# Block products for six of the eight gate columns of the second half's last merge

## The chip, the cores and the metric

The kernel runs on one core of one Trainium2 chip. The core has five engines with a queue each: TensorE (PE: matmuls, with its weight loads shown as PEld), VectorE (DVE), ScalarE (ACT), GpSimd (POOL) and SyncE (SP, which here only issues DMAs). Each engine works through its own queue in order; between engines they wait on semaphores. The metric is the device time of one execution in microseconds, the median of the runs.

## The reference

One layer of a conditioned decoder runs over a prompt of 1024 tokens and over 8 samples of 4 tokens each, with shared weights and a model width of 1024. All arithmetic is in float32.

```
h = rmsnorm(x, norm1_g) * (1 + sc1) + sh1
u = h @ w_in                     # u_x, u_g, u_q, u_k, u_v, u_r, u_lr, u_ga, u_gb
y_a = rg_lru(causal_conv(u_x)) * gelu(u_g)
y_b = headnorm(gla(u_q, u_k, u_v, u_lr)) * silu(u_r)
m = sigmoid(u_ga) * (y_a @ proj_a) + sigmoid(u_gb) * (y_b @ proj_b)
x = x + gt1 * (m @ w_out)
h2 = rmsnorm(x, norm2_g) * (1 + sc2) + sh2
x = x + gt2 * ((silu(f1) * f2) @ ffn_w2)      # f1, f2 = halves of h2 @ ffn_w1
y = rmsnorm(x, final_g)
```

The change concerns the line of `m`, in it the first gate: `sigmoid(u_ga)`, where `u_ga = h @ w_in[:, ga]` has 1024 columns, that is eight tiles of 128.

## The kernel before

**Halves.** Features lie on the 128 partitions, tokens along the free dimension. The work is done in two halves one after the other: half A has 512 prompt tokens, half B the other 512 and the 32 sample tokens (544 columns, of which a matmul takes two pieces of 272). Names of tiles end in `a` or `b` accordingly.

**Split products.** A float32 matrix product is made of three passes in the type fp32r. Weights (`split_w`) and inputs (`split`) are each split into a high part (a copy by ScalarE) and a rest (a subtraction by VectorE); `gemm` adds high x high, high x rest and rest x high in PSUM. A plain gate column of half B is therefore 8 tiles of the inner dimension x 2 pieces x 3 = 48 matmuls of 272 columns; its `proj_a` column, with an inner dimension of 1280 = 10 tiles, is 60.

**Block products.** The first FFN matrix is multiplied in another way (`ffn1_fast` with `products` and `block_sums`): weights (two column tiles) and inputs (two halves of the inner dimension, two halves of the tokens) are seen as 2 x 2 blocks, and seven products of blocks, after sums on both sides, take the place of eight. The sums of the weights are made beforehand by VectorE and kept in DRAM (`weight_sums`, `late_sums`, into `wsum`), the sums of the inputs by `block_sums`: four rounds, each with two additions over all tokens, four subtractions over half of them and three splits. A round's temporaries `d0`, `d1`, `ta`, `tb` come from a pool of six buffers (tag "t"); its results `t12` and every second round's `t4` from a pool of 17 (tag "S"). The first product, "11", needs no sums of the inputs; the second, "t1", needs the `t12` of all four rounds.

**The stages of half B.** `branches` runs the attention (`gla`) with a list of other work as its fill, in this order: values of the first pair of heads, queries and keys of the second, values of the second, the `r` tiles, the LRU branch (`lru`). Then comes `merge_b` (eight columns of the second gate and of `proj_b`), with the LRU's remaining steps woven in; then `merge_a` (eight columns of the first gate and of `proj_a`); then `back`: out-projection, second norm, FFN. Between `merge_a` and `back` the PSUM pool is changed from three tiles of two banks to six of one (`mm_pool(1)`).

**The weight sums.** `late_sums` is a list of jobs, each in two steps. The first step has POOL copy one column of the tile in `pace[0]`, the latest gate, which makes its queue wait until that is written, and then issue two loads; the second has VectorE do four additions and POOL issue two stores. `merge_b` takes two steps per column from its fifth column on, `merge_a` two steps per column: 24 steps for 12 jobs.

**Order.** A scheduler orders each engine's instructions at build time, by program order and by when it expects their inputs. A piece of code under `high_priority` is moved ahead (the weight splits by 70 instructions); `as_written` fixes the order of one engine from a given place on, which the block products use for PE.

## Time and profile before

| | us |
|---|---|
| median of three runs (lowest, highest) | 1967.7 (1966.91, 1968.15) |
| the profiled execution | 1969.03 |
| span of its profile | 1967.3 |
| second merge of half B, `merge_a`: first gate matmul to first matmul of the out-projection | 1429.06 to 1539.00 |

Times in the trace are counted from the start of the span. One instruction's duration includes the time in which the next one already runs: a matmul of 272 columns is listed with some 0.29 us although the next follows after 0.12. So rates are read from start to start. A line of the profile names the line of the kernel, the engine, the tile written and the tiles read; "idle before" and the name behind an arrow say how long the engine stood still and what ended that.

### The profile page before, as it was taken

Reading aid. Unit: us, or ns where it says so; the run is one execution under the profiler, and the core shown is the slowest. Engines: PE = TensorE matmul, PEld = TensorE weight load, DVE = VectorE, ACT = ScalarE, POOL = GpSimd, SP = SyncE. Lnnn points to the kernel's source line nnn. Section 1 sums busy time; section 2 is a strip of 40 time slices with the busy share of each in tenths; the row PEclk is TensorE's granted clock in tenths of the full one; section 3 lists DMA queues with packets and bytes.
Section 4 is the critical chain, followed back from the end, with each engine's and each line's share of the span. In section 5 each row is a group of like instructions: output and inputs, shape, how many; then the busy total and the mean of one; then the engine's idle time right before and its main releaser. Section 6 shows DMA issues by size and latency. Waiting matters only on the chain. (4 is left out here: it accounts for less than half of the span.)

```text
span 1967.3 us, 33687 instructions
## 1 busy us (share of the span) xinstructions
PE 1935.1 (98%) x13428; PEld 1762.0 (90%) x13428; DVE 1320.0 (67%) x2293; ACT 942.8 (48%) x1442; POOL 107.5 (5%) x231
## 2 busy tenths in 40 slices
PE   8999999999999999999999999999999999999998
PEld 5877877777899998998899999899999999999997
DVE  5638487655558765778564597684365588888867
ACT  4645375533235542555353355563232344566653
POOL 0000001000000000000000001010221000000000
PEclk9999999999999999999999999999999999999999
DMA  8334235567644457554422313323456544555553
GB/s 340 98 106 156 81 107 193 186 229 277 219 164 143 149 187 247 179 174 142 157 76 89 116 60 108 102 82 107 135 198 216 202 135 129 173 169 179 176 163 108
DMA packets 116797, 307.68 MB, mean 156 GB/s; under 512 B 13728, under 2 KB 28832, under 8 KB 116640
## 3 DMA queue, kind: packets, MB, share of 16 engines
q1 hardware_dynamic: 104656, 260.74, 40.8%
q0 software_dynamic: 11440, 44.23, 6.1%
q8 instruction: 105, 1.72, 0.4%
q10 hardware_dynamic: 544, 0.56, 0.1%
q14 instruction: 52, 0.43, 0.1%
HBM read 271.08 MB, written 34.39 MB: 155 GB/s over the span
## 5 line engine op out<-in xcount | busy, mean ns | idle before, releaser
L151 DVE TENSOR_TENSOR fwa_hl<-fwa,fwa_hl 128x1024 fp32r<-128x1024 f32 (+1 forms) x57 | 68.8, 1206 | 44.7 <-ACT fwa_hl L150 41.2
L151 DVE TENSOR_TENSOR fwb_hl<-fwb,fwb_hl 128x1024 fp32r<-128x1024 f32 (+1 forms) x64 | 77.2, 1206 | 27.8 <-ACT fwb_hl L150 25.7
L150 ACT ACTIVATE fwa_hl<-fwa 128x1024 fp32r<-128x1024 f32 (+1 forms) x57 | 59.3, 1040 | 43.9 <-PE fapsa L1338 10.7
L150 ACT ACTIVATE fwb_hl<-fwb 128x1024 fp32r<-128x1024 f32 (+1 forms) x64 | 66.6, 1041 | 23.5 <-PE fcpsb L1338 9.1
L438 PE MATMUL f3psa<-faa,f3a_hl 128*128 128x512 f32 x176 | 68.6, 390 | 0.6 <-ACT f3a_hl L150 0.6
L440 PE MATMUL f3psa<-faa,f3a_hl 128*128 128x512 f32 x176 | 68.5, 390 | 0.4 <-DVE f3a_hl L151 0.4
L439 PE MATMUL f3psa<-faa,f3a_hl 128*128 128x512 f32 x176 | 68.6, 390 | 0.0
L150 ACT ACTIVATE f3a_hl<-f3a_raw 128x768 fp32r<-128x768 f32 (+1 forms) x32 | 25.3, 792 | 55.6 <-PE f3psa L440 47.3
L438 PE MATMUL uxpsb<-h1b,uxpsb_hl 128*128 128x256 f32 (+1 forms) x160 | 47.9, 299 | 0.1
L439 PE MATMUL uxpsb<-h1b,uxpsb_hl 128*128 128x256 f32 (+1 forms) x160 | 46.7, 292 | 0.0
L440 PE MATMUL uxpsb<-h1b,uxpsb_hl 128*128 128x256 f32 (+1 forms) x160 | 46.4, 290 | 0.0
L438 PE MATMUL ugpsb<-h1b,ugpsb_hl 128*128 128x272 f32 x160 | 46.3, 289 | 0.0
L440 PE MATMUL ugpsb<-h1b,ugpsb_hl 128*128 128x272 f32 x160 | 46.1, 288 | 0.0
L439 PE MATMUL ugpsb<-h1b,ugpsb_hl 128*128 128x272 f32 x160 | 45.8, 286 | 0.0
L438 PEld LDWEIGHTS f3psa<-faa,f3a_hl 128*128 128x128 f32 x176 | 33.1, 188 | 7.8 <-ACT f3a_hl L150 1.0
L440 PEld LDWEIGHTS f3psa<-faa,f3a_hl 128*128 128x128 f32 x176 | 33.0, 188 | 7.6 <-DVE f3a_hl L151 0.9
L151 DVE TENSOR_TENSOR f3a_hl<-f3a_raw,f3a_hl 128x768 fp32r<-128x768 f32 (+1 forms) x32 | 28.2, 887 | 16.4 <-ACT f3a_hl L150 16.3
L439 PEld LDWEIGHTS f3psa<-faa,f3a_hl 128*128 128x128 f32 x176 | 33.0, 188 | 6.7
L438 PE MATMUL wopsb<-mb,wob_hl 128*128 128x272 f32 x128 | 36.8, 288 | 1.1 <-DVE gab L1203 1.1
L438 PE MATMUL rpsb<-h1b,rpsb_hl 128*128 128x272 f32 x128 | 37.8, 295 | 0.0
L438 PE MATMUL vpsb<-h1b,vpsb_hl 128*128 128x272 f32 x128 | 37.4, 293 | 0.0
L439 PE MATMUL rpsb<-h1b,rpsb_hl 128*128 128x272 f32 x128 | 37.4, 292 | 0.0
(1134 smaller groups left out, 7739.5 us busy)
## 6 DMA issues: line engine op xcount, KB each, us to landing
ada<-in_ada_w SPq DMA_DIRECT2D x48, 512.0 KB, 6.0
fwb<-wsum SPq DMA_DIRECT2D x72, 256.0 KB, 3.4
s_raw<-in_ffn SPq DMA_DIRECT2D x32, 512.0 KB, 3.5
wsum<-s_raw POOLq DMA_DIRECT2D x32, 512.0 KB, 3.3
fwa<-wsum SPq DMA_DIRECT2D x64, 256.0 KB, 3.3
fwb<-in_ffn SPq DMA_DIRECT2D x54, 256.0 KB, 3.4
fwa<-in_ffn SPq DMA_DIRECT2D x48, 256.0 KB, 3.2
woa_raw<-in_w_out SPq DMA_DIRECT2D x13, 512.0 KB, 3.5
```

Of the source, the lines that this page charges most:

```text
L150: act.activation(hl[:, 0, :n], raw[:, :n], AF.Copy)
L151: dve.tensor_sub(hl[:, 1, :n], raw[:, :n], hl[:, 0, :n].bitcast(F32))
L438: pe.matmul(out, wh, x[:, o:o + w], start=st, stop=False)
L439: pe.matmul(out, wh, x[:, N + o:N + o + w], start=False, stop=False)
L440: pe.matmul(out, wl, x[:, o:o + w], start=False, stop=en)
```

## The change

Couples of columns (2, 3), (4, 5) and (6, 7) of half B's first gate are made by block products (`gates_fast`), columns 0 and 1 stay plain. `block_sums` now takes the tiles to be summed as an argument; for the normed input `h` its four rounds are traced one by one: behind the gate and behind the `proj_a` of columns 0 and 1. The splits of the merged columns `m` are traced later: column 0 behind column 1, columns 1 to 5 behind the last couple's gates. Three couples of gate columns add six jobs ahead of the others in `late_sums`, 18 jobs with 36 steps in all; twelve steps are taken one by one in the fill of the attention, two per column in `merge_b` from its third column on, the rest in `merge_a`. In these jobs the first addition is put behind VectorE's latest traced instruction (`behind`). The change of the PSUM pool stands at the beginning of `merge_a`. The gate tiles of `w_in` are stored with the tiles of the inner dimension in the order `KORD`, for half A as well, where they are still multiplied plainly, and half A's merge adds into `mb` in place of `ga`.

```diff
 KORD = (0, 2, 4, 6, 1, 3, 5, 7)
+GATES = (1, 2, 3)
...
     def traced():
         return nc.cur_bb.bb.instructions
+
+    def behind(n):
+
+        now = list(traced())
+        mine = [i for i in now[max(0, n - 4000):n] if i.engine == now[-1].engine]
+        order = mybir.DependencyInfo(mybir.DependencyClass.NoSync, mybir.DependencyReason.DATA)
+        tc.add_manual_dep(now[-1], mine[-1].name, order, reason="as written")
 
     def as_written(begin, engines):
 
...
     wsum = {f: drp.tile([P, 2048], F32, name=f"wsum{f}") for f in range(FAST[1], NF)}
+    wsumg = {c: drp.tile([P, 2048], F32, name=f"wsumg{c}") for c in GATES}
     wsum2 = {(q, g): drp.tile([P, 1536], F32, name=f"wsumf{q}{g}") for q in range(4) for g in range(2)}
 
     def S(name, dt=F32):
...
 
         jobs = []
         halves = lambda t, u, c: t.rearrange("p (n u) -> p n u", n=2)[:, :, c * u:(c + 1) * u]
-        for f in range(FAST[1], FAST[0]):
+        couples = [(wsumg[c], [I["w_in"][T_GA + 2 * c + v] for v in range(2)]) for c in GATES]
+        couples += [(wsum[f], [I["ffn1"][2 * f + v] for v in range(2)]) for f in range(FAST[1], FAST[0])]
+        for sums, src in couples:
             for c in range(2):
-                to = [halves(wsum[f][:, v * 1024:(v + 1) * 1024], 256, c) for v in range(2)]
-                jobs.append((256, [halves(I["ffn1"][2 * f + v], 256, c) for v in range(2)], to))
+                to = [halves(sums[:, v * 1024:(v + 1) * 1024], 256, c) for v in range(2)]
+                jobs.append((256, [halves(t, 256, c) for t in src], to))
         for g in range(2):
             for q in range(4):
                 c = P * (4 + 6 * g)
...
                 pool.dma_start(rv[v], src[v])
             yield 1
             r1, r2 = rv
+            last = len(traced())
             dve.tensor_add(r2[:, 1], r2[:, 0], r2[:, 1])
+            behind(last)
             dve.tensor_sub(r2[:, 0], r1[:, 0], r2[:, 0])
             dve.tensor_sub(r1[:, 0], r2[:, 1], r1[:, 0])
             dve.tensor_sub(r1[:, 1], r1[:, 1], r1[:, 0])
...
             yield 1
 
     sums_of, sums_late = weight_sums(), late_sums()
+
+    def paced(g, jobs):
+        for w in g:
+            next(jobs, None)
+            yield w
 
     class Half:
         def __init__(s, hf):
...
                 ps, hl = s.early.pop(t)
                 s.gemm(ps, hl, 4, s.h, 4, False, True, hk=4)
                 return ps
-            ps = mm(name)
-            s.gemm(ps, w_in_tile(t, name), KD, s.h, split=split)
+            ps = s.wide(name) if T_GA <= t < T_GB else mm(name)
+            s.gemm(ps, w_in_tile(t, name), KD, s.h, split=split, order=KORD if T_GA <= t < T_GB else None)
             return ps
 
         def by_tiles(s, dst, i, ps, func, **kw):
...
             for i in range(2):
                 ps = s.proj_h(T_Q + 2 * pr + i, f"qps{n}{i}", s.tiled)
                 s.by_tiles(q, i, ps, AF.Copy, scale=float(128 ** -0.5))
+                pace[0] = q
                 yield 5.2
             for i in range(2):
                 h = 2 * pr + i
...
             for i in range(2):
                 ps = s.proj_h(T_K + 2 * pr + i, f"kps{n}{i}", s.tiled)
                 s.by_tiles(k, i, ps, AF.Copy)
+                pace[0] = k
                 yield 5.2
             box += [z, q, k]
 
...
                     ps = s.proj_h(T_V + 4 * pr + 2 * i + c, f"vps{n}{i}{c}")
                     vf = T(f"vf{n}{i}{c}")
                     act.activation(s.sv(vf[:, :N]), s.pv(ps), AF.Copy)
+                    pace[0] = vf
                     if pend:
                         tp_(*pend)
                     pend = (i, c, vt, vs, vf)
...
                 pace[0] = tg
                 if s.hf == 0 and j:
                     next(sums_of, None)
-                elif s.hf and j >= 4:
+                elif s.hf and j >= 2:
                     next(sums_late, None)
                     next(sums_late, None)
                 yield 5.2
 
+        def over(s, t, ps):
+
+            return [(s.sv(t[:, :s.N]), s.pv(ps))] if s.hf == 0 else [(t[:, s.cols(p)], s.psv(ps, p)) for p in s.parts]
+
+        def gate_a(s, j):
+            n = f"{s.n}{j}"
+            ps = s.proj_h(T_GA + j, "gaps" + n)
+            tg = T("ga" + n)
+            for t, p in s.over(tg, ps):
+                act.activation(t, p, AF.Tanh, scale=0.5)
+            pace[0] = tg
+            return tg
+
+        def gates_fast(s, c, product):
+
+            N, W = s.N, s.N // 2
+            hi, lo = slice(0, W), slice(W, N)
+            pa, pb, pc = [mm(f"h{k}ps{s.n}{c}")[:, 0, :W] for k in "abc"]
+            v1, v2 = T(f"gc{s.n}{c}"), T(f"gd{s.n}{c}")
+            product(pa, "11", True)
+            s.snap(v1[:, lo], pa)
+            product(pb, "t1", True)
+            s.snap(v2[:, lo], pb)
+            product(pa, "t2", False)
+            s.snap(v1[:, hi], pa)
+            product(pb, "22", False)
+            product(pa, "t3", False)
+            s.snap(v2[:, hi], pa)
+            dve.tensor_add(v1[:, hi], v1[:, hi], pb)
+            product(pc, "21", True)
+            dve.tensor_add(v1[:, lo], v1[:, lo], pc)
+            dve.tensor_add(v2[:, hi], v2[:, hi], v2[:, lo])
+            act.activation(v1[:, :N], v1[:, :N], AF.Tanh, scale=0.5)
+            product(pa, "t4", False)
+            act.activation(v2[:, lo], pa, AF.Tanh, scale=0.5)
+            act.activation(v2[:, hi], v2[:, hi], AF.Tanh, scale=0.5)
+            pace[0] = v1
+            return v1, v2
+
+        def proj_a(s, j, tg):
+            n, N = f"{s.n}{j}", s.N
+            p2 = s.wide("paps" + n)
+            s.gemm(p2, load_w(I["proj_a"][2 * j], 640, "pa0" + n), 5, s.y_a, 0, True, False)
+            s.gemm(p2, load_w(I["proj_a"][2 * j + 1], 640, "pa1" + n), 5, s.y_a, 5, False, True)
+            for t, p in s.over(tg, p2):
+                dve.scalar_tensor_tensor(t, t, 1.0, p, op0=OP.add, op1=OP.mult)
+            dve.tensor_add(s.mb[j][:, :N], tg[:, :N], s.mb[j][:, :N])
+
+        def keep_m(s, *js):
+            for j in js:
+                m = S(f"m{s.n}{j}", F32R)
+                split(m, s.mb[j][:, :s.N], s.N)
+                s.m.append(m)
+
         def merge_a(s):
-            N, mb = s.N, s.mb
             s.m = []
-            for j in range(KD):
-                n = f"{s.n}{j}"
-                ps = s.proj_h(T_GA + j, "gaps" + n)
-                tg = T("ga" + n)
-                act.activation(s.sv(tg[:, :N]), s.pv(ps), AF.Tanh, scale=0.5)
-                pace[0] = tg
-                if s.hf:
+            if s.hf == 0:
+                for j in range(KD):
+                    s.proj_a(j, s.gate_a(j))
+                    s.keep_m(j)
+                    if j % 3 < 2 and j < 7:
+                        next(sums_of, None)
+                return
+            mm_pool(1)
+            b = s.block_sums(s.h, "h")
+            for j in range(2):
+                tg = s.gate_a(j)
+                next(b)
+                next(sums_late, None)
+                s.proj_a(j, tg)
+                next(b)
+                next(sums_late, None)
+            drain(b)
+            s.keep_m(0)
+            units = []
+            for c in GATES:
+                w1, w2, sm = I["w_in"][T_GA + 2 * c], I["w_in"][T_GA + 2 * c + 1], wsumg[c]
+                units += [w1[:, 0:512], sm[:, 1536:2048], sm[:, 0:512], sm[:, 512:1024], sm[:, 1024:1536], w1[:, 512:1024],
+                          w2[:, 512:1024]]
+            begin = len(traced())
+            product = s.products(units, 512, s.bs, "gw" + s.n)
+            for c in GATES:
+                tgs = s.gates_fast(c, product)
+                next(sums_late, None)
+                if c == GATES[-1]:
+                    s.keep_m(*range(1, 2 * c))
+                for i in range(2):
+                    s.proj_a(2 * c + i, tgs[i])
+                    if c == GATES[-1]:
+                        s.keep_m(2 * c + i)
                     next(sums_late, None)
-                p2 = mm("paps" + n)
-                s.gemm(p2, load_w(I["proj_a"][2 * j], 640, "pa0" + n), 5, s.y_a, 0, True, False)
-                s.gemm(p2, load_w(I["proj_a"][2 * j + 1], 640, "pa1" + n), 5, s.y_a, 5, False, True)
-                dve.scalar_tensor_tensor(s.sv(tg[:, :N]), s.sv(tg[:, :N]), 1.0, s.pv(p2), op0=OP.add, op1=OP.mult)
-                dve.tensor_add(tg[:, :N], tg[:, :N], mb[j][:, :N])
-                m = S("m" + n, F32R)
-                split(m, tg[:, :N], N)
-                s.m.append(m)
-                if s.hf:
-                    next(sums_late, None)
-                elif j % 3 < 2 and j < 7:
-                    next(sums_of, None)
+            as_written(begin, (mybir.EngineType.PE,))
 
...
-        def block_sums(s):
+        def block_sums(s, hs, tag=""):
 
             N, W = s.N, s.N // 2
             s.bs = {k: [] for k in ("11", "21", "22", "t1", "t2", "t3", "t4")}
             t3 = t4 = None
             for i in range(4):
-                h0, h1 = s.h2[2 * i], s.h2[2 * i + 1]
-                d0, d1, ta, tb = [T(f"{c}{s.n}{i}") for c in ("d0", "d1", "ta", "tb")]
+                h0, h1 = hs[2 * i], hs[2 * i + 1]
+                d0, d1, ta, tb = [T(f"{c}{tag}{s.n}{i}") for c in ("d0", "d1", "ta", "tb")]
                 for d, h in (d0, h0), (d1, h1):
                     dve.tensor_add(d[:, :N], h[:, :N].bitcast(F32), h[:, N:2 * N].bitcast(F32))
                 dve.tensor_sub(ta[:, :W], d0[:, :W], d0[:, W:N])
...
         def back(s):
             s.x, s.h2 = [], []
             p0, p1 = s.halves
-            if s.hf:
-                mm_pool(1)
             a0, a1 = [ACC("20" + s.n)], [ACC("21" + s.n)]
             drain(s.out_proj(p0, a0))
             o1 = s.out_proj(p1, a1)
...
             next(f)
             mix(s.norm2(p1, a1), f)
             drain(f)
-            b = s.block_sums()
+            b = s.block_sums(s.h2)
             if s.hf == 0:
                 mix(chain(s.ffn1_first(p1, EARLY), s.ffn1(range(EARLY, FAST[0]))), b)
                 drain(b)
...
             r = weave(s.r_tiles(), s.adas, 2)
             l = s.lru()
             fill = chain(g0, f, g1, r, l)
+            if s.hf:
+                fill = paced(fill, islice(sums_late, 4 * len(GATES)))
             mix(s.gla(0, *b0, g0, v0), fill)
             drain(f)
             mix(side(s.gla(1, *b1, g1, v1), s.head_norm(0)), fill)
...
         col(f["final_g"])], axis=1))
     w = f["w_in"][0]
     o = np.cumsum([0, 1280, 1280, 512, 512, 1024, 1024, 16, 1024, 1024])
-    a["w_in"] = _tiles(np.concatenate([w[:, :o[6]], w[:, o[7]:]], 1))
+    wi = _tiles(np.concatenate([w[:, :o[6]], w[:, o[7]:]], 1))
+    wg = wi[T_GA:T_GB].reshape(T_GB - T_GA, P, KD, P)[:, :, list(KORD)]
+    wi[T_GA:T_GB] = wg.reshape(T_GB - T_GA, P, D)
+    a["w_in"] = wi
     wl = np.zeros((P, KD, P), np.float32)
     wl[:, :, 0:16] = w[:, o[6]:o[7]].reshape(KD, P, 16).transpose(1, 0, 2)
     for o in (32, 64, 96):
```

More of the change, by code (lines that the diff above doesn't have):

```diff
@@ L1 @@
 from contextlib import ExitStack
+from itertools import islice
 import concourse.bass as bass
@@ L1300, in block_sums @@
                 if i == 0:
-                    t3 = pair(tp.tile([P, 2 * 544], F32R, tag="m2t", name="t3" + s.n, bufs=1))
+                    t3 = pair(tp.tile([P, 2 * 544], F32R, tag="m2t", name="t3" + tag + s.n, bufs=1))
                 if i == 2:
-                    t3 = [tp.tile([P, 544], F32R, tag="acc", name=f"t3{c}{s.n}", bufs=2) for c in "hl"]
+                    t3 = [tp.tile([P, 544], F32R, tag="acc", name=f"t3{c}{tag}{s.n}", bufs=2) for c in "hl"]
                 if i % 2 == 0:
-                    t4 = pair(S(f"t4{s.n}{i}", F32R))
-                t12 = pair(S(f"t12{s.n}{i}", F32R))
+                    t4 = pair(S(f"t4{tag}{s.n}{i}", F32R))
+                t12 = pair(S(f"t12{tag}{s.n}{i}", F32R))
                 o4 = i % 2 * W
```

## The prediction

> **What bounds the kernel now.** I read the page first, then the windows of the stage that the diff touches, and the time lines of TensorE, VectorE and ScalarE there.
>
> ```profile
> span 1967.3 us, 33687 instructions
> ...
> PE 1935.1 (98%) x13428; PEld 1762.0 (90%) x13428; DVE 1320.0 (67%) x2293; ACT 942.8 (48%) x1442; POOL 107.5 (5%) x231
> ```
>
> ```profile
> core 0: us, PE busy (x) PEld busy (x) DVE busy (x) ACT busy (x) POOL busy (x), PEclk, DMA share, GB/s
> 1175.00:1180.00 5.00, 4.40 (x16) 3.81 (x17) 2.63 (x7) 0.87 (x2) 0.33 (x2) 0.66 0.18 72
> 1420.00:1425.00 5.00, 5.00 (x43) 5.00 (x42) 2.37 (x4) 1.57 (x3) 1.84 (x5) 1.00 0.51 170
> 1425.00:1430.00 5.00, 5.00 (x42) 5.00 (x42) 1.36 (x4) 4.94 (x6) 1.02 (x2) 1.00 0.59 209
> 1429.00:1442.50 13.50, 13.20 (x106) 12.98 (x106) 9.95 (x20) 5.19 (x8) 4.56 (x9) 1.00 0.26 87
> 1442.50:1456.00 13.50, 13.19 (x105) 12.97 (x106) 8.87 (x12) 4.21 (x6) 4.57 (x8) 1.00 0.67 222
> 1469.30:1482.70 13.40, 13.40 (x110) 13.40 (x109) 7.01 (x10) 3.71 (x5) 2.54 (x6) 1.00 0.72 257
> 1540.00:1545.00 5.00, 5.00 (x42) 5.00 (x42) 3.02 (x5) 2.04 (x3) 0.17 (x1) 1.00 0.61 214
> 1666.00:1740.00 74.00, 74.00 (x594) 74.00 (x593) 57.64 (x93) 43.68 (x72) 0.00 (x0) 1.00 0.53 163
> 990.00:1045.00 55.00, 54.85 (x482) 53.44 (x480) 37.78 (x68) 30.09 (x53) 0.00 (x0) 1.00 0.25 76
> 1045.00:1090.00 45.00, 45.00 (x362) 42.15 (x361) 18.36 (x43) 12.15 (x21) 1.08 (x2) 1.00 0.30 98
> ```
>
> TensorE is busy in 98% of the span, so time is gained only by giving it fewer matmuls or by closing one of its gaps. Columns of the windows: length, then busy time and count of PE, PEld, DVE, ACT, POOL, then the granted clock, DMA share and GB/s. The last merge of the second half runs from 1429.06 to about 1538. From 1469 on TensorE is busy without a break while VectorE has half its time free. In the first two columns (1429 to 1456) VectorE works 18.8 us of 27, because the tail of the LRU branch runs there.
>
> ```profile
> 1429.06 0.29 PE L438 MATMUL gapsb<-h1b,gapsb_hl 128*128 128x272 f32 x1
> ...
> 1441.76 0.29 PE L438 MATMUL papsb<-yab,pa1b_hl 128*128 128x272 f32 x1
> 1442.35 0.39 PE L439 MATMUL papsb<-yab,pa1b_hl 128*128 128x272 f32 x1 [0.30 <-DVE yab L185]
> ...
> 1443.20 0.29 PE L439 MATMUL gapsb<-h1b,gapsb_hl 128*128 128x272 f32 x1
> 1443.80 0.39 PE L440 MATMUL gapsb<-h1b,gapsb_hl 128*128 128x272 f32 x1 [0.31 <-DVE gapsb_hl L151]
> ...
> 1537.62 0.29 PE L440 MATMUL papsb<-yab,pa1b_hl 128*128 128x272 f32 x1
> 1539.00 0.36 PE L438 MATMUL wopsb<-mb,wob_hl 128*128 128x272 f32 x1 [1.10 <-DVE gab L1203]
> ```
>
> ```profile
> 1490.15 0.63 ACT L1196 ACTIVATE gab<-gapsb 128x544 f32<-128x544 f32 x1 [2.04 <-PE gapsb L440]
> ...
> 1503.60 0.63 ACT L1196 ACTIVATE gab<-gapsb 128x544 f32<-128x544 f32 x1 [2.53 <-PE gapsb L440]
> ```
>
> The two tanh of consecutive columns lie 13.45 us apart. One column is 48 matmuls of 272 columns for the gate and 60 for `proj_a`: 13.45/108 = **124.5 ns** a matmul. The time line of PE shows three small gaps, which I read from start to start: 0.59 us at `yab` and 0.60 at `gapsb_hl` instead of 0.12, together 0.95 lost, and 1.38 at the first `wopsb`, on `gab`: 1.26 lost.
>
> **What the change removes.** A couple of plain gate columns is 96 matmuls; by block products it is 7 products of 4 x 3 = 84. Three couples save 36 x 0.1245 = **4.48 us**. The window 1666 to 1740 holds the same block-product structure in the first FFN matrix, with this half's 272-wide blocks: PE is busy 74.00 of 74.00 us with DVE at 57.6. So the snapshots, the additions and the 3.5 weight splits per couple (2 before) don't hold TensorE up; I price them at 0. If that cover were gone, the bound is one split's 1.14 us per product pair; the windows speak against it, since in the loop over couples VectorE has some 17 us of work in 25.4 (204 matmuls x 0.1245).
>
> The 1.26 us at the first `wopsb` goes too: it is the change of PSUM pools, which `mm_pool(1)` now makes before the stage. There the first gate must wait for the last `mbb` (0.7 us, row below); below it turns out that this is covered.
>
> **What it adds: the block sums.** They need VectorE before the second product, "t1", of the first couple, since that reads all four `t12`. Undisturbed, TensorE would reach it at 1429.06 + (216 + 12) x 0.1245 = **1457.4**. Nothing can be put ahead of it: PE's order is written down from there. What must VectorE do by then?
>
> ```profile
> 1431.52 0.42 DVE L379 TENSOR_TENSOR sums<-sums 128x256 f32<-128x256 f32 x1 [3.91 <-DMA sums<-in_ffn]
> 1431.98 0.42 DVE L380 TENSOR_TENSOR sums<-sums,sums 128x256 f32<-128x256 f32 x1
> ...
> 1433.24 0.71 DVE L1179 SCALAR_TENSOR_TENSOR mbb<-gbb,pbpsb 128x544 f32<-128x544 f32 x1
> 1433.87 1.35 DVE L1095 TENSOR_TENSOR tib<-tib,lmb 128x544 f32<-128x544 f32 x2
> ...
> 1441.57 0.72 DVE L185 TENSOR_TENSOR yab<-ggb,yab 128x544 fp32r<-128x544 f32 x1 [0.72 <-ACT yab L184]
> 1442.52 1.23 DVE L151 TENSOR_TENSOR gapsb_hl<-gapsb_raw,gapsb_hl 128x1024 fp32r<-128x1024 f32 x1 [0.22 <-ACT gapsb_hl L150]
> 1443.66 0.82 DVE L151 TENSOR_TENSOR pa0b_hl<-pa0b_raw,pa0b_hl 128x640 fp32r<-128x640 f32 x1
> ...
> 1460.60 0.56 DVE L379 TENSOR_TENSOR sums<-sums 128x384 f32<-128x384 f32 x1 [5.39 <-DMA sums<-in_ffn]
> 1461.19 0.56 DVE L380 TENSOR_TENSOR sums<-sums,sums 128x384 f32<-128x384 f32 x1
> 1462.86 0.71 DVE L1203 SCALAR_TENSOR_TENSOR gab<-gab,papsb 128x544 f32<-128x544 f32 x1
> 1463.49 0.82 DVE L151 TENSOR_TENSOR pa1b_hl<-pa1b_raw,pa1b_hl 128x640 fp32r<-128x640 f32 x1
> 1464.22 0.72 DVE L1204 TENSOR_TENSOR gab<-gab,mbb 128x544 f32<-128x544 f32 x1
> ```
>
> ```profile
> L1294 DVE TENSOR_TENSOR d0b<-h2b 128x544 f32<-128x544 f32 x4 | 2.9, 715 | 0.0
> ...
> L1311 DVE TENSOR_TENSOR t12b<-tab,t12b 128x544 fp32r<-128x544 f32 x4 | 2.9, 715 | 0.0
> ...
> L1296 DVE TENSOR_TENSOR tab<-d1b,tab 128x272 f32<-128x272 f32 x4 | 1.7, 433 | 0.0
> ...
> L1311 DVE TENSOR_TENSOR t4b<-tbb,t4b 128x272 fp32r<-128x272 f32 x4 | 1.7, 430 | 0.0
> ```
>
> Rows overlap by about 0.08 us (a 715 ns addition is followed 0.63 us later), so I count start to start. Block sums, from the four rounds in the FFN: per round 3 operations of 0.715 and 6 of 0.43 us (`d1b`, `tbb` and `t3b` are as wide as the rows shown); four rounds are 12 x 0.715 + 24 x 0.43 = 18.9 less 36 x 0.08 = 16.0 us; without the last t3 and t4, which t1 doesn't need, **15.3**. Beside them stand, from 1429.3 (last `pbpsb` written): the last `mbb` 0.64; one job of weight sums, four times 0.59 = 2.4; the LRU tail, 1433.87 to 1442.29 less a `pa1b` split (0.74) and an idle 0.72 = 7.0; the splits of one `pa1b` (0.74), `gapsb` (1.14), two of `pa` (1.5) and the first couple's weights (1.14); column 0's two outputs 1.3. That is 15.9. With the block sums 31.2: VectorE ends at **1460.5** if it never idles. The next job of weight sums is traced ahead of the third round and its data are there by then: 2.4 more, 1462.9. With a second split of the couple's weights (1.14) and column 1's outputs (1.3) ahead of the last round it is 1465.3.
>
> In the other direction, VectorE idles 3.91 us before the row of 1431.52, which a job's DMA ends, and 6.3 of 10 us from 1420 to 1430. `behind` puts that job after `mbb`, so this wait no longer holds the tail up. But the block sums' temporaries come from the six buffers of tag "t", and until the LRU's last products two each of its tiles `tib` and `ggb`, with the gate's, hold five; only the first two additions (1.3 us) have room to go early: 1459.2 is the early end.
>
> I take **1462.9**, the order of the program: t1 comes 5.5 us late. In it are contained the pool change's 0.7 and the old 0.95, which both lie before.
>
> **The clock.** TensorE's one wait of 2.45 us before 1175.6 (on `attb`, the row follows) is followed by a granted clock of 0.66 for 5 us, 1.7 us lost; after the 1.26 us at 1539 it stayed 1.00. A wait of over 4 us at t1 (5.5 less what was lost before it) is the former kind: **+1.7**; 0 at the early end.
>
> ```profile
> 1175.60 1.62 PE L836 MATMUL spsb<-wb 128*128 128x128 f32 x6 [2.45 <-DVE attb L853]
> ```
>
> [...]
>
> **The moved weight sums.** Six jobs more (three couples), and twelve of the now 36 steps run among the values, keys and queries. There, 990 to 1090, PE idles 0.15 us in 100 and DVE has 44 us free for 6 x 4 x 0.46 = 11 (1431.52 to 1431.98); POOL has worked 1.1 us, and the LRU's copies come behind it. Each load is issued one step (5 us of matmuls or more) ahead of its additions. Price 0. What is queued behind a late one on VectorE is the level work of the attention; TensorE's one long wait there, 2.45 with its clock 1.7, is the price of one that is not covered, and up to two of them bound it: 0 to 8. Below nothing: fewer additions stand in the merge's columns only after 1456, where nothing waits; so no gain. DMA: a couple loads seven half tiles of 0.25 MB of gate weights instead of four (SP issues two each), but fewer sums fall into the stage; at a share of 0.72 of its engines TensorE didn't wait. The m splits, put off to the last couple (7 x 0.64 = 4.5 us beside 15 us of `proj_a`), and the reordered gate weights cost nothing either; for the last m the out-projection has other columns to do, as now.
>
> **The sum.** 5.5 (late t1) - 0.95 (old gaps) - 4.48 (matmuls) - 1.26 (pool) + 1.7 (clock) = **+0.5 us**. The profiled execution took 1969.03 us with its span of 1967.3; the median of the runs is 1967.7, 1.3 less. The difference goes onto the median: **1968.2**. Bounds of the block sums: early 1.8 - 6.69 = -4.9; late 7.9 - 6.69 + 1.7 = +2.9.
>
> **Rivals.** First, *the block sums are hidden*: what VectorE does in the first two columns is done early enough, because more of the first rounds falls into its idle time before 1429. For it: 6.3 us free from 1420 to 1430. Against it: the five tiles held. From an end before 1460.2 on the time is over 0.2% better; fully hidden only the pool's 0.7 stays: 0.7 - 6.69 = -6.0, **1961.7**.
>
> Second, slower: *the temporaries start only when the LRU tail is over*, and that is as late as now, at 1442.3, because VectorE, in order, still waits for a job's DMA ahead of it. Then 15.3 + splits 4.9 + outputs 2.6 + a job 2.4 = 25.2 follow, end 1467.5, t1 10.1 us late: 10.1 - 6.69 + 1.7 = +5.1, **1972.8**. It decides from an end after 1466.3 on. For it: 24 us of VectorE's waits of this kind in this stage in the row below; against it: `behind`.
>
> ```profile
> DVE sums L379 <- DMA sums<-in_ffn: 24.7, 9, 5.4
> ```
>
> Third, slower: *the moved jobs break into the attention*: one uncovered wait, 2.45 + 1.7, on the forecast: +4.7, **1972.4**. Against it: PE idles 0.15 us there although it has the same kind of neighbours on VectorE.
>
> Fourth, that the block products don't save what they say: with a gap per product they would gain nothing; the window 1666 to 1740 excludes it.
>
> **Chances.** A measurement here tells about 0.2% (3.9 us) from no change. Forecast 0.48 (ends from 1460.2 to 1466.3, all within 0.2%); hidden 0.28, faster; late temporaries 0.16 and broken attention 0.08, slower. So faster 0.28, same 0.48, slower 0.24. The range reaches from the hidden case to the late temporaries: 1961.5 to 1973.0; the forecast's own is 1964 to 1971.5.
>
> **What would show it.** Right: 84 gate matmuls per couple, 124.5 ns apart; VectorE without idle time from 1429 to t1; one wait of PE at "t1" of the first couple on a `t12`, of 3 to 5 us, a granted clock under 1 behind it, and no gap at the first `wopsb`. Wrong: no wait there (the sums were early), waits at later products (the splits are not covered), or idle PE between 990 and 1090.

## The result, and the profile after

The changed kernel takes **1980.3 us** (median; 1976.88 to 1982.88), the kernel before 1967.9 beside it: ratio **1.0058**, 95% interval 1.0047 to 1.0069. It is slower by 0.6%, where no change was forecast. The profiled execution took 1980.42 us with a span of 1978.6; the profile of before took 1969.03.

The page of after, the head of its first part (span; busy time of each engine):

```profile
span 1978.6 us, 33840 instructions
...
PE 1932.4 (98%) x13392; PEld 1758.8 (89%) x13392; DVE 1353.3 (68%) x2375; ACT 957.8 (48%) x1476; POOL 138.6 (7%) x267
```

TensorE has 36 matmuls fewer (13428 before), as the diff says; the share of 98% looks the same. The time is found by places. For each kernel I read from the tile views where the second half's first matmul stands (`lrpsb`), where the `r` columns begin (`rpsb`), where the last `pbpsb` is issued and where the first `wopsb` begins. That makes three lengths: the first half, the attention (`lrpsb` to `rpsb`) and the last merge (`pbpsb` to `wopsb`). They are those of the one profiled execution; the median is that of all runs of the version, and the ratio is to the kernel before, run beside it.

| kernel | first half ends | attention | last merge | median | ratio, 95% interval |
|---|---|---|---|---|---|
| before | 960.1 | 128.4 | 110.1 | 1967.4 to 1968.7 | |
| after | 961.6 | **136.5** | **114.6** | 1980.3 | 1.0058, 1.0047 to 1.0069 |
| e1_moved_alone | 960.1 | 136.5 | 111.8 | 1976.1 | 1.0041, 1.0027 to 1.0054 |
| e2_sums_in_a | 965.3 | 128.4 | 114.4 | 1980.2 | 1.0056, 1.0043 to 1.0069 |
| e3_four_plain | 962.6 | 136.2 | 109.1 | 1978.1 | 1.0046, 1.0033 to 1.0060 |
| e4_no_jobs_plain | 960.4 | 134.6 | 123.4 | 1988.7 | 1.0103, 1.0089 to 1.0117 |
| e5_no_pace | 964.1 | 128.4 | 114.4 | 1973.1 | 1.0030, 1.0019 to 1.0042 |
| e6_later_steps | 961.8 | 130.4 | 116.1 | 1976.2 | 1.0045, 1.0032 to 1.0057 |
| e7_proj_first | 961.5 | 135.1 | 108.0 | 1973.5 | 1.0022, 1.0012 to 1.0032 |
| e8_both | 960.5 | 129.9 | 107.9 | 1968.2 | 1.0005, 0.9996 to 1.0014 |
| e9_no_pace_proj | 963.5 | 128.4 | 107.6 | 1967.3 | 0.9996, 0.9987 to 1.0005 |
| e10_const_plain | 961.8 | 129.1 | 112.0 | 1973.4 | 1.0030, 1.0020 to 1.0040 |
| e11_jobs_behind | 961.4 | 128.4 | 105.3 | 1968.5 | 1.0002, 0.9994 to 1.0011 |
| e12_one_earlier | 961.6 | 129.1 | **105.0** | **1966.0** | 0.9989, 0.9981 to 0.9998 |

So the changed kernel's span, 11.3 us longer, is: first half +1.5, attention +8.1, merge +4.5, the rest +0.5, and 3.3 that come back between the `r` columns and the merge. The view of waits of after, TensorE's rows (in total, times, longest):

```profile
PE hbpsb L1427 <- ACT t12hb L1401: 5.8, 1, 5.8
PE spsb L852 <- DVE vs L714: 4.6, 1, 4.6
...
PE vtrb L719 <- DVE vs L714: 1.3, 1, 1.3
...
PE gapsb0l L457 <- ACT pa1b_hl L160: 0.9, 1, 0.9
...
PE hbpsb L1428 <- DVE t12hb L1402: 0.8, 1, 0.8
```

None of the five stands in the profile of before, and the gap at the first `wopsb` is gone. The windows of after (columns as in the prediction):

```profile
990.00:1045.00 55.00, 49.08 (x416) 47.67 (x415) 34.08 (x62) 25.96 (x41) 12.05 (x16) 0.94 0.33 106
1028.00:1033.00 5.00, 4.13 (x48) 3.98 (x49) 3.99 (x9) 2.61 (x6) 0.85 (x2) 0.50 0.54 162
1435.30:1448.80 13.50, 12.28 (x97) 11.88 (x96) 11.44 (x23) 5.83 (x9) 5.36 (x11) 1.00 0.41 139
1448.80:1462.30 13.50, 13.40 (x106) 12.96 (x105) 13.42 (x28) 6.07 (x11) 4.83 (x3) 1.00 0.64 197
...
1466.40:1480.00 13.60, 7.04 (x42) 6.51 (x41) 11.46 (x21) 4.82 (x10) 3.28 (x5) 0.75 0.50 153
...
1677.00:1751.00 74.00, 74.00 (x593) 74.00 (x593) 57.64 (x92) 43.53 (x72) 0.00 (x0) 1.00 0.54 162
```

From 990 to 1045 PE does 416 matmuls where it did 482, and behind its wait at `spsb` the granted clock is 0.50 for five us. In the merge VectorE is full (13.42 of 13.50) until t1. From 1466.4 to 1480 PE does 42 matmuls, 5.2 us of work at 124.5 ns each, in 13.6: 6.6 us are waits, and the 1.8 that are left are the lower clock's. The FFN's window is unchanged, as it should be.

**The attention.** The time line of VectorE there, and that of GpSimd:

```profile
1018.39 1.20 DVE L161 TENSOR_TENSOR qpsb_hl<-qpsb_raw,qpsb_hl 128x1024 fp32r<-128x1024 f32 x1
1026.21 0.42 DVE L392 TENSOR_TENSOR sums<-sums 128x256 f32<-128x256 f32 x1 [6.62 <-DMA sums<-in_w_in]
...
1027.94 0.68 DVE L819 TENSOR_TENSOR wb<-bcb 128x512 f32<-128x512 f32 x1
1028.54 0.27 DVE L714 COPY vs<-vtqb 32x128 f32<-32x128 f32 x1
```

```profile
1016.09 3.67 POOL L387 COPY sums<-vfb 128x1 f32<-128x1 f32 x2 [6.04 <-ACT vfb L733]
1019.95 1.42 POOL L388 DMA_DIRECT2D sums<-in_w_in  x2 [0.19 <-POOL sums L387]
```

VectorE was ready for the second job's additions at 1019.6. Their two loads had been issued only from 1019.95 on, because a GpSimd copy, which first waits for the newest `vfb` (6.04 us) and then takes 3.67 for the two tiles, stands ahead of them; the data came at 1026.2. Behind the additions stood `wb` and `vs`, and TensorE waited for `vs`.

**The merge.** VectorE's time line, then PE's at t1:

```profile
1435.55 0.72 DVE L1201 SCALAR_TENSOR_TENSOR mbb<-gbb,pbpsb 128x544 f32<-128x544 f32 x1 [1.66 <-PE pbpsb L459]
...
1439.43 0.56 DVE L392 TENSOR_TENSOR sums<-sums 128x384 f32<-128x384 f32 x1 [1.81 <-DMA sums<-in_ffn]
...
1448.06 0.71 DVE L195 TENSOR_TENSOR yab<-ggb,yab 128x544 fp32r<-128x544 f32 x1
...
1468.92 0.44 DVE L1256 SCALAR_TENSOR_TENSOR gab<-gab,papsb1l 128x272 f32<-128x272 f32 x1 [1.11 <-POOL sums L387]
...
1474.08 0.71 DVE L1402 TENSOR_TENSOR t12hb<-tahb,t12hb 128x544 fp32r<-128x544 f32 x1
```

```profile
1473.47 0.59 PE L1427 MATMUL hbpsb<-t12hb,gwb_hl 128*128 128x272 f32 x1 [5.78 <-ACT t12hb L1401]
1474.84 0.60 PE L1428 MATMUL hbpsb<-t12hb,gwb_hl 128*128 128x272 f32 x1 [0.78 <-DVE t12hb L1402]
```

The stage begins at 1435.2. `behind` did put the job's additions behind the last `mbb`, and they wait for their DMA there, 1.81 us, within the LRU tail, which ends with the second `yab` at 1448.7: 13.5 us after the begin; in the kernel before it was 13.4 (1442.3 after 1428.9). From there it is 26.1 us to the last `t12` (1474.8), 1.11 of them a wait for a GpSimd copy, the rest work. That is 39.6 us after the begin.

Where the 3.3 us come back: the same stretch of 963 matmuls, from the last `r` column to shortly before the first `pbpsb`, in the kernel before and in after:

```profile
1154.00:1290.00 136.00, 130.16 (x963) 122.20 (x963) 104.95 (x205) 79.25 (x121) 15.95 (x44) 0.96 0.31 98
```

```profile
1163.60:1296.30 132.70, 126.92 (x964) 119.33 (x963) 104.93 (x205) 79.29 (x121) 15.94 (x44) 0.99 0.32 101
```

The engines beside TensorE do the same work; its clock is granted at 0.99 instead of 0.96. Cut into stretches of 4 us, five of 34 lie under 0.95 in before and two of 33 in after; why is open.

### The profile page after: what moved, and what is told of

It is laid out like the page before. It is cut to its first block, busy times and chain, and to the rows that moved or that the text cites. A ratio compares the mean times of both kernels' runs of the same rounds, so it can differ in the third digit from the quotient of the medians.

```text
span 1978.6 us, 33840 instructions
## 1 busy us (share of the span) xinstructions
PE 1932.4 (98%) x13392; PEld 1758.8 (89%) x13392; DVE 1353.3 (68%) x2375; ACT 957.8 (48%) x1476; POOL 138.6 (7%) x267
## 5 line engine op out<-in xcount | busy, mean ns | idle before, releaser
L358 DVE TENSOR_TENSOR s_raw<-s_raw 128x512 f32<-128x512 f32 x16 | 11.1, 691 | 41.9 <-DMA s_raw<-in_ffn 41.8
L457 PE MATMUL rpsb<-h1b,rpsb_hl 128*128 128x272 f32 x128 | 37.8, 295 | 0.0
L457 PE MATMUL vpsb<-h1b,vpsb_hl 128*128 128x272 f32 x128 | 37.4, 292 | 0.0
L458 PE MATMUL rpsb<-h1b,rpsb_hl 128*128 128x272 f32 x128 | 37.4, 292 | 0.0
```

The source lines that it names most:

```text
L358: dve.tensor_add(r2[:, 512:1024], r2[:, 0:512], r2[:, 512:1024])
L457: pe.matmul(out, wh, x[:, o:o + w], start=st, stop=False)
L458: pe.matmul(out, wh, x[:, N + o:N + o + w], start=False, stop=False)
```

## The experiments

Two theories. *Two losses*: the moved jobs break the attention, the late block sums break the merge, each by itself. *One cause*: VectorE's arrears from the attention, or another part of the change (wide PSUM tiles, reordered weights), cost both.

**e1_moved_alone**: the plain merge, the jobs of gate sums still made.

```diff
-            mm_pool(1)
-            b = s.block_sums(s.h, "h")
-            for j in range(2):
+            for j in range(KD):
...
+                s.keep_m(j)
```

> The merge is plain again (eight gate columns of 48 matmuls, PSUM pools changed where they were before), but the six jobs of gate weight sums are made, twelve steps of them in the attention and the rest in the last merge; nobody reads the sums. Output unchanged. Theory A (the moved jobs alone break the attention: a late job DMA of 6.6 us and slow POOL copies stand ahead of the vs and wb tiles): the wait of PE at spsb on vs near 1028 is there again, rpsb's last matmul comes 6 to 9 us later than in the kernel before, and the time is 1971 to 1976. Theory B (the moved jobs cost nothing by themselves; the loss in the attention comes from another part of the change, such as the wide PSUM tiles or the new order of the gate weights): rpsb as before within 1.5 us, time 1967 to 1969.

Theory A: the attention takes 136.5 us again with nothing of the block products in the kernel. Its merge is 1.7 longer than before, with a wait of 2.8 at `papsb`.

**e2_sums_in_a**: the gate sums in the first half.

```diff
+        of += [(wsumg[c], I["w_in"][T_GA + 2 * c], I["w_in"][T_GA + 2 * c + 1]) for c in GATES]
...
-                    if j % 2 == 0:
+                    if j < 7:
...
-            if s.hf:
-                fill = paced(fill, islice(sums_late, 4 * len(GATES)))
```

> The gate weight sums are made in the first half, as whole couples among the FFN's second matrix, and nothing is threaded through the attention of the second half; the merge keeps its block products, with the same eight late steps in its first two columns. Theory A (two separate losses): no wait at spsb on vs beyond the 2.5 us that the kernel before has, rpsb's last matmul within 3 us of the kernel before, about 5 us less at the end than the changed kernel, 1973 to 1976; the wait at hbpsb in the first couple stays at 5 us or more. Theory B (one cause: the merge is late because the attention is late and VectorE still holds its arrears): the wait at hbpsb shrinks below 2 us as well, time 1962 to 1969. If the first half pays for the three couples, its end (lrpsb's first matmul) is over 1.5 us later than in the changed kernel.

The attention is whole again (128.4), so wide PSUM tiles and reordered weights cost nothing there; the merge is as long as in after, with the same 5.8 us at `hbpsb`. Hence two losses. The time is no better: in this profile the first half ends 3.7 us later than in after. TensorE's waits at `f3psa`, between 700 and 965, are 4.7 us there, against 1.0 in before and 2.0 in after:

```profile
PE f3psa L460 <- DVE f3a_hl L161: 3.2, 5, 1.2
PE f3psa L458 <- ACT f3a_hl L160: 1.5, 3, 0.6
```

**e3_four_plain**: `GATES = (2, 3)`, four plain columns first.

> Four plain gate columns ahead instead of two, and two couples of block products; four gate jobs instead of six, still eight steps in the attention. Theory A (t1 waits because the block sums end about 39 us after the stage begins, whatever stands ahead on TensorE): with four plain columns t1 would be reached after 54 us, so no wait at hbpsb and no dip of the clock; the merge takes 432 + 2 x 204 = 840 matmuls of 0.1245 us = 104.6 us and a little, against 109.9 (1429.1 to 1539.0) in the kernel before, 1.26 of the difference being the change of pools; together with some loss in the attention 1968 to 1973. Theory B (the block sums follow VectorE's other work and are pushed back by the additional columns too): a wait over 2 us at hbpsb again and 1975 to 1981.

t1 starts at 1497.7 and waits for nothing, although the last `t12` is again ready only 37.4 us after the begin: the late block sums, not the products, make the wait in the merge. Its 109.1 us are still 4.5 above 840 x 0.1245; waits at `papsb2l` (1.0), at the first gate (0.9) and at `hapsb` (0.7) are 2.6 of that.

**e4_no_jobs_plain**: the late steps out of the two plain columns, two behind each `proj_a` instead.

> The changed kernel with the two late steps taken out of the two plain columns (they follow later, two after each proj_a in the couples). Theory A (the job's DMA wait of 1.8 us, its four additions of 0.6 us and the POOL copy of 3.7 us that VectorE waits 1.1 us for are a large part of t1's lateness): t12 is ready 5 to 6 us earlier, the wait at hbpsb falls from 5.8 us to under 1.5 and the clock no longer dips, 1973 to 1976. Theory B (the lateness is the LRU tail and the temporaries that it holds; the job only fills time that VectorE would idle): the wait stays over 4 us, 1979 to 1981.

Both theories missed. The last `t12` comes 37.2 us after the begin (39.6), but the steps now stand in pairs in the couples, a load and behind it its additions. PE's waits, and VectorE's time line at the one at `hapsb`:

```profile
PE hbpsb L1426 <- ACT t12hb L1400: 4.1, 1, 4.1
PE papsb6l L459 <- DVE pa0b_hl L161: 2.9, 1, 2.9
PE hapsb L1428 <- DVE gwb_hl L161: 2.9, 1, 2.9
```

```profile
1523.57 0.56 DVE L392 TENSOR_TENSOR sums<-sums 128x384 f32<-128x384 f32 x1 [5.79 <-DMA sums<-in_ffn]
1524.04 1.22 DVE L161 TENSOR_TENSOR gwb_hl<-gwb,gwb_hl 128x1024 fp32r<-128x1024 f32 x1
```

The additions wait 5.79 us for their DMA, the split of `gwb` stands behind them in the list, and TensorE waits for it. The merge is 8.8 us longer than in after. Behind the wait of 4.1 TensorE's matmuls follow 0.23 us apart from 1469.1 to 1473.2, instead of 0.12, and again from 1525.7 to 1527.3 behind that at `hapsb`.

**e5_no_pace**: the loads not held to q, k and v tiles.

```diff
-                pace[0] = q
+                pace[0] = vec
```

(the same for `k` and `vf`.)

> The changed kernel, with the loads of the moved jobs no longer held to the newest q, k or v tile (the GpSimd copy that stands ahead of each load reads a constant instead), so they go out as soon as their buffers are free, some 5 to 8 us earlier. Theory A (the loads are late, and VectorE, in order, stands behind their DMA): VectorE's waits on these DMAs, 19.2 us for six jobs in the changed kernel, fall under 6, the wait of PE at spsb on vs falls from 4.6 us to under 1.5, rpsb's last matmul comes within 4 us of the kernel before (9.6 in the changed kernel), 1973 to 1976. Theory B (VectorE's additions by themselves, or GpSimd's copies beside a busy VectorE, hold the attention up): the wait at spsb stays above 3 us, 1978 to 1982.

Theory A for the attention, in full: the same six jobs at the same place, and 128.4 us. The window of after shown above, here:

```profile
990.00:1045.00 55.00, 54.85 (x482) 53.50 (x482) 40.87 (x76) 32.74 (x51) 13.23 (x19) 1.00 0.38 125
```

and the second job's loads and additions, on GpSimd and VectorE:

```profile
1013.48 0.71 POOL L388 DMA_DIRECT2D sums<-in_w_in  x1 [0.31 <-POOL sums L387]
...
1014.68 0.72 POOL L388 DMA_DIRECT2D sums<-in_w_in  x1 [0.30 <-POOL sums L387]
```

```profile
1018.91 0.41 DVE L392 TENSOR_TENSOR sums<-sums 128x256 f32<-128x256 f32 x1
```

Issued some 6 us earlier, although this second half starts 2.5 us later, they let the additions start without a wait. VectorE's waits for such loads fell only to 13.4 us, not under 6, but those that are left stand where nothing waits. The total gained 7.2 us against after.

**e6_later_steps**: the moved steps begin four steps of the fill later (`if i >= 4` in `paced`).

> The changed kernel, with the moved jobs' steps begun four steps of the fill later (behind the first pair's values), where VectorE has 29 us of 100 busy from 1040 to 1060 in the kernel before. Theory A (the loss in the attention is one of place: jobs among the first pair's values, whose vs and wb tiles TensorE needs at once): no wait over 2.6 us between 990 and 1090, rpsb's last matmul within 3 us of the kernel before, 1973 to 1976. Theory B (the jobs cost wherever they stand in the attention): the waits reappear at the second pair's tiles or in the rps columns, 1978 to 1982.

Theory A in the main: 130.4 us, without the wait at `spsb` on `vs`; 2 us are left, with small waits at `pob` (1.3) and `rpsob` (0.4). The last `rpsb` comes 5.1 us later than in before, not within 3; 1.7 of that is the first half's.

**e7_proj_first**: 60 matmuls of `proj_a` ahead of t1.

```diff
             for c in GATES:
+                p2 = [s.proj_mm(2 * c) if c == GATES[0] else None, None]
                 tgs = s.gates_fast(c, product)
...
-                    s.proj_a(2 * c + i, tgs[i])
+                    s.proj_a(2 * c + i, tgs[i], p2[i])
```

(`proj_mm` holds the loads and matmuls of `proj_a`, which now takes their result.)

> The changed kernel, with the 60 matmuls of column 2's proj_a put ahead of the first couple's block products, which puts t1 off by 60 x 0.1245 = 7.5 us of TensorE's work; same matmuls, same jobs, same block sums. Theory A (t1 waits only for block sums that end some 39 us after the stage begins): the 5.8 and 0.8 us at hbpsb and the dip of the clock go, first wopsb comes about 7 us earlier against the stage's begin (107 to 109 us behind the last pbpsb instead of 114.6), 1973 to 1976. Theory B (VectorE is short in the whole stage, so that work put ahead brings its own splits and the wait moves on): waits of 3 us or more at papsb, hapsb or hbpsb, 1978 to 1981.

Theory A: 108.0 us, no wait at `hbpsb`, the clock at 1.00. The last `t12`, the stage's window, and PE's waits in it:

```profile
1471.15 0.72 DVE L1408 TENSOR_TENSOR t12hb<-tahb,t12hb 128x544 fp32r<-128x544 f32 x1
```

```profile
1433.20:1541.20 108.00, 104.82 (x832) 103.66 (x831) 83.64 (x146) 45.98 (x77) 25.47 (x44) 1.00 0.67 219
```

```profile
PE hapsb L1435 <- DVE gwb_hl L161: 2.2, 2, 1.6
PE gapsb0l L457 <- ACT pa1b_hl L160: 0.9, 1, 0.9
```

The block sums end as late as ever, 38.7 us after the begin (1433.2). TensorE has something else to do meanwhile; only the splits of `gwb` are now late by 2.2 us.

**e8_both**: e6 and e7 together.

> The edits of the two runs before together: moved jobs four steps later, column 2's proj_a ahead of the first couple. If the two losses are separate and each edit takes its own away, their gains add: 1980 less 6 less 6, 1966 to 1970, as fast as the kernel before or faster by up to 0.1%; with 36 matmuls and the change of pools saved in full it would be 1962 to 1964. If one feeds the other, or a third loss of the same size stands behind, 1972 to 1976.

The gains add: 1968.2. **e9_no_pace_proj** takes e5 in place of e6.

> The attention's loads unpaced (as in e5_no_pace) and column 2's proj_a ahead of the first couple (as in e7_proj_first) together. If the two losses are separate, rpsb's last matmul comes as late as lrpsb's first against the kernel before (no loss between them), the merge takes 108 us from the last pbpsb to the first wopsb instead of 110.1, and the time is 1963 to 1967, the fastest so far. If the unpaced loads only moved their cost into the later columns, 1968 to 1971.

Attention 128.4, merge 107.6: the two losses are separate, and their cures too. The total, 1967.3, missed the 1963 to 1967 by a little; in the profiled execution, which took 1969.3, the first half ends 3.4 us later than in before.

**e10_const_plain**: e9, `pace[0] = vec` in the plain columns too.

> e9_no_pace_proj with the loads of weight sums in the two plain columns unpaced as well: GpSimd's copy ahead of each load reads a constant and not the gate's tile gab. Theory A (the jobs cost the stage their late DMA, 1.8 us, and the 1.1 us that VectorE waits for a GpSimd copy of 3.7 us that reads gab): the last t12 is ready about 35 us after the stage begins instead of 38 to 39.6, the waits at hapsb on gwb_hl (2.1 us in e7 and e8) go, 1 to 3 us faster than e9_no_pace_proj. Theory B (the additions themselves, 2.2 us a job, and the splits make the lateness): under 1 us of difference, VectorE's lateness as before.

Neither: the last `t12` comes 36.8 us after the begin (37.8 in e9), and then the next job's additions wait for their DMA ahead of a `gwb` split. VectorE's row, then PE's, then GpSimd's two ahead of that DMA:

```profile
1470.24 0.56 DVE L392 TENSOR_TENSOR sums<-sums 128x384 f32<-128x384 f32 x1 [3.75 <-DMA sums<-in_ffn]
```

```profile
PE hapsb L1435 <- DVE gwb_hl L161: 5.1, 1, 5.1
```

```profile
1461.25 5.29 POOL L387 COPY sums<-vec 128x1 f32<-128x1 f32 x1
1466.84 0.54 POOL L388 DMA_DIRECT2D sums<-in_ffn  x1 [0.30 <-POOL sums L387]
```

The copy no longer waits for a tile, but the load behind it went out later, not earlier: 37.1 us after the begin, in e9 31.9. In e9 VectorE's write to `gab` had to wait for the GpSimd copies of `gab` (1.11 us), and in that pause they ended. Here nothing stopped VectorE until 1466.50, and the copy, begun at 1461.25, ended at 1466.54. What matters is still whether additions stand in the list before their data are there.

**e11_jobs_behind**: e9 without additions in the plain columns; three steps behind the last column.

```diff
-                next(sums_late, None)
+                if j == 0:
+                    next(sums_late, None)
...
+            for _ in range(3):
+                next(sums_late, None)
             as_written(begin, (mybir.EngineType.PE,))
```

(the step behind `proj_a` of the plain columns is gone.)

> e9_no_pace_proj with the additions of weight sums taken out of the two plain columns: one load stays there, its additions come in the first couple, and three steps follow behind the stage's last column. Theory A (VectorE's work ahead of t1 is what counts: one job's 2.2 us and the wait for GpSimd's copy): the last t12 is ready 34 to 36 us after the stage begins, the first couple waits for nothing, 1 to 3 us faster than e9_no_pace_proj. Theory B (as in e4_no_jobs_plain, what is put off collides with the couples or the out-projection): new waits of 2 us or more, 0 to 4 us slower than e9_no_pace_proj.

Both, one behind the other: the last `t12` 33.0 us after the begin (1461.8), the merge 105.3, and then the out-projection loses 4.0 us, with a wait on its weights:

```profile
PE wopsb L459 <- DVE wob_hl L161: 1.8, 1, 1.8
```

**e12_one_earlier**: those three steps taken away, one job more in `merge_b` (`j >= 1` for `j >= 2`).

> e11_jobs_behind with one job of weight sums more in merge_b (from its second column on instead of the third), so that the three steps behind the stage's last column fall away. Theory A (e11 gains 4.9 us up to the out-projection and gives 4 back there, through VectorE and the wait on wob_hl of 1.8 us that the steps behind cause): the stage again ends 4 to 5 us earlier against its begin than in the kernel before, nothing is given back, 1962 to 1965, faster than the kernel before by 0.1 to 0.25%. Theory B (the additional job stands among the LRU's last tiles, where VectorE is full, or the out-projection is late for another reason): first pbpsb later by 2 us or more, or wopsb waiting again, 1967 to 1970.

Theory A: nothing is given back. The last merge of the kernel before, and of e12:

```profile
1428.90:1539.00 110.10, 108.40 (x867) 107.76 (x866) 63.54 (x97) 32.94 (x44) 24.65 (x54) 1.00 0.62 211
```

```profile
1430.80:1535.80 105.00, 103.85 (x832) 103.44 (x831) 79.26 (x138) 46.34 (x77) 19.59 (x35) 1.00 0.62 201
```

5.1 us are saved, and TensorE's one wait of over 0.2 us left there is that at the first gate, 0.9. The time, 1966.0, is a little above the 1962 to 1965 expected, and the interval of its ratio (0.9981 to 0.9998) lies just below 1: the first of the twelve versions that is faster than the kernel before, by 0.1%, in one set of runs.

## Why the prediction was wrong

*Matmul price and saving (4.48 us): right.* In e12 the merge saves 5.1 us: 4.48, the pool's 1.26 and the old gaps' 0.95, less the 0.8 of the pool's new place, are 5.9; 0.8 of that didn't come.

*The pool change costs 0.7 at the first gate: right*, 0.9 less the usual 0.12.

*The products' snapshots, sums and splits are covered: right in after,* where no product behind t1 waits. But e4 and e10 show how thin the cover is: one job's additions, late and ahead of a split, cost 2.9 and 5.1 us at `hapsb`.

*t1 is late by 5.5 us: wrong; the second rival had the mechanism, in the main.* The step that failed is "I take 1462.9, the order of the program", and ahead of it "`behind` puts that job after `mbb`, so this wait no longer holds the tail up". It moved the job from one place ahead of the tail to one within it, and the tail still ended as late as in the kernel before. From the stage's begin to the last `t12` the forecast had 34.0 us (1428.9 to 1462.9), the rival 13.4 + 25.2 = 38.6; measured 39.6. VectorE's two waits, 1.81 for the job's DMA and 1.11 for a GpSimd copy, are 2.9 of the 5.6 us over the forecast. The rest is work that stood ahead of the last `t12` as well: column 1's outputs and a second split of `gwb`, which the forecast kept for its late end, and a third split, which it had nowhere.

The rival's price for the merge was +5.1, measured +4.5, the clock's 1.8 (1.7 forecast) included. It came out lower although the sums were later: t1's first nine matmuls need only the first three `t12` and ran ahead of the wait, 1.1 us that neither the forecast nor the rival took off. e3 and e7 keep TensorE from waiting for the sums, and 5.5 and 6.6 us of the merge come back, in e3 with one couple of block products less. The additions in the plain columns are a part of the lateness: e9 and e11 differ there only, up to t1, and have 37.8 and 33.0 us. In e4, without them, but with 2.17 us of waiting for a job's DMA in the tail and three splits of `gwb` ahead, it was 37.2.

*The clock: right in size* (1.8 us in the merge, 1.7 forecast), but the length of a wait doesn't decide it alone. The wait at `spsb` on `attb` is 2.45 us long in after too (before 1185.16); the granted clock behind it is 1.00 there (1185 to 1190), and 0.66 in before.

*The moved weight sums cost nothing: wrong.* The step that failed is "Each load is issued one step (5 us of matmuls or more) ahead of its additions. Price 0". The step in the program was ahead, the load was not: its GpSimd copy waited for a tile of that same step, and load and additions met on the chip with 4.8 us of DMA between them. The prediction read DMA times for `sums` from the merge and didn't follow the pace copy. The third rival named the mechanism, but with one wait of 2.45 and 1.7 of clock; it was 4.6 and 1.3 of waits, and the 2.2 that are left of the 8.1 are the clock's. e1, e2 and e5 show it.

*The rivals shut each other out: wrong.* They stand in different stages and both came, so the upper end of the range (1973.0), which holds one of them, fell short. The merge missed its +0.5 by 4.0 us and the attention its 0 by 8.1; with 1.5 of the first half, 0.5 of the rest and the 3.3 that come back these make the 11.3.

*Open:* the first half. Its end varies by up to 5.2 us among these profiles; in e5 it is 4.0 longer than before, and 4.5 of that stood there already at its FFN (`f1psa`). Except in e2 no run tells what of it is the change's and what is the execution's. Nor is it known why the granted clock between the stages is better in after: e1, e4 and e7, with a late attention, gain 3.4 to 4.0 us there too, but e3, with 136.2, only 0.3. No run takes `behind` away or gives the temporaries more buffers, so what either does to the tail by itself is not shown.

## What to carry to other kernels

A job that is threaded into an in-order engine's list costs time where its data are not there when the engine gets to it and needed work stands behind it: here VectorE's waits of 6.62 (after), 5.79 (e4) and 3.75 us (e10) stood ahead of TensorE's of 4.6, 2.9 and 5.1, and in e5 the same jobs cost the attention nothing (128.4 us). So follow each load back to what holds its issue, a pace copy or a buffer, and compare that with the DMA's own time (in after 3 to 5 us from the end of the second issue to the additions). Where operands of a product come late, look first for independent work of the same engine to put ahead of it; in e7 the 6.6 us of waits at `hbpsb` went although the last `t12` came 38.7 us after the begin instead of 39.6. Risks that stand in different stages add (here 8.1 and 4.5 us): the range has to hold their sum.

## What the runs showed of the hardware

A GpSimd copy of one column of `gab` took 0.19 us in before (median of 16; longest 1.13), but up to 3.74 in after, and one of `vec` 5.29 in e10. Beside each of these two VectorE worked without a pause until 0.04 us before its end (1453.30 and 1466.50). The tile view of `sums`, GpSimd's copies, in the kernel before and in after (ns: shortest, median, longest):

```profile
L375 POOL COPY sums<-gab x16: 174/186/1134, 1441.6 to 1531.3; 128x1 f32<-128x1 f32 x16
```

```profile
L387 POOL COPY sums<-gab x4: 196/2146/3742, 1447.0 to 1468.7; 128x1 f32<-128x1 f32 x4
L387 POOL COPY sums<-gbb x12: 175/185/672, 1354.9 to 1435.5; 128x1 f32<-128x1 f32 x12
```

In the time line of after, two long ones and a short one behind them, and VectorE at the end of the first:

```profile
1449.60 3.74 POOL L387 COPY sums<-gab 128x1 f32<-128x1 f32 x1 [1.21 <-DMA wsumf<-sums]
...
1464.15 3.71 POOL L387 COPY sums<-gab 128x1 f32<-128x1 f32 x1 [0.51 <-DMA wsumf<-sums]
...
1468.69 0.20 POOL L387 COPY sums<-gab 128x1 f32<-128x1 f32 x1
```

```profile
1452.59 0.71 DVE L1385 TENSOR_TENSOR d0hb<-h1b 128x544 f32<-128x544 f32 x1
1453.38 0.44 DVE L1256 SCALAR_TENSOR_TENSOR gab<-gab,papsb0l 128x272 f32<-128x272 f32 x1
```

The first ended at 1453.34, in the short break of VectorE between 1453.30 and 1453.38, after six VectorE instructions that began later than it; the next in VectorE's list writes `gab`, which this copy reads. The copies of 1016.09 and 1464.15 also end within 0.2 us of the start of a break, and that of 1461.25 in e10 outlasted nine instructions. But the copy of 1446.97 ended after 0.58 us, beside a single one and without a break, so what makes a copy long is not shown. VectorE paid 1.11 us for the copy of 1464.15 (the row of 1468.92): its write to `gab` waits for the next copy of `gab`, that of 1468.69, which had to queue behind it.
